# Seven products of a pair collected in one PSUM bank, with ScalarE copies between them

## The chip, the cores and the metric

The kernel runs on one core of a Trainium2 chip. The metric is the device time of one execution in microseconds (us). TensorE (PE) multiplies, VectorE (DVE) adds and subtracts, ScalarE (ACT) casts, copies and evaluates functions, GpSimd (POOL) and SyncE (SP) here mainly issue DMAs. Each engine runs its own list of instructions in order, and lists wait for one another by semaphores.

## The reference

One decoder block over x of 1024 tokens by 1024 channels in float32. What is computed, cut to its core:

```
h = rms_norm(x, norm_g)
proj = h @ w_in          # u, g_rnn, q, k, v, g_attn, m_rnn, m_attn
y_rnn  = rg_lru(conv4(u)) * silu(g_rnn)
y_attn = sliding_window_attention(rope(q), rope(k), v, sinks) * silu(g_attn)
merged = sigmoid(m_rnn) * (y_rnn @ w_rnn_out) + sigmoid(m_attn) * (y_attn @ w_attn_out)
out = rms_norm(x + merged @ w_o, final_norm_g)
```

## The kernel before

**Products.** A float32 product is made of three float32r matmuls: each operand is split into a high part (an ACT cast, L427) and a low part (a DVE subtraction, L428), and high by high, high by low, low by high are summed in PSUM (L508 to L510). Each matmul is 128 rows by 512 columns. The weights come in pairs of 128-column units. A `Pair` is a product of a 256 by 1024 by a 1024 by 1024 matrix in 2 by 2 blocks, done by Strassen's scheme in Winograd's form: seven block products instead of eight, each of 4 x 3 matmuls (`product`), so 84 matmuls a pair. Left factors are A11, A12, A22, S1, S2, S3, S4 (S1 to S4 are sums of blocks, by DVE), right factors B11, B21, T2, T3, T1, T4, B22 (T1 to T4 are sums of the right matrix's blocks, also made and split on DVE and ACT, once for all pairs of that right matrix).

**One pair.** `Pair.run` uses five PSUM banks a to e. Product 0 (A11 B11) goes to a, and ACT copies it to SBUF (`p1`, L517). Product 1 (S2 T2) goes to b, and DVE adds the copy: u2 = b + c1. Product 2 (A12 B21) goes onto a, which then is the first result block. Product 3 (S3 T3) goes to c: u3 = c + u2. Product 4 (S1 T1) goes to d: c22 = d + u3. Product 5 (A22 T4) goes to e: c21 = e + u3. Product 6 (S4 B22) goes onto d, after c22 has read it: c12 = d + u2. All the additions are DVE's (L435).

**Stages.** After the norm and the transposes of x (right matrix h), two pairs of the merge gate are done in the plain form (`fd`). Then 24 pairs run over h: `ug` (u and g_rnn together, followed by the recurrence `lru`), `mr`, `ma`, `ga` (gates), `k`, `v`, `q`. Between them stand the 32 attention units `a00` to `a37` (scores, softmax on ACT and DVE, values). Then come four pairs `zr` with y_rnn as the right matrix and four pairs `za` with y_attn as the right matrix (`z_seven`, `comb_from`: y is loaded back from DRAM, for `za` also multiplied by the gate sg, `YB`; then T1 to T4 are made and 28 buffers are split). `z_tail` multiplies each result by its gate (`tz`) and adds both branches. Last is the product with w_o (`o`), the residual, the norm and the store.

**What sets the order.** `Plan` records every operation with what it reads and writes, and places them one after another on the engines by estimated times, priorities (`prio` with offsets such as `lru`, `ztl`, `comb`) and counts of buffers allowed per class (`raw`, `wc`, `B`, `Y`, `ld`). `TUNE['orders']` gives the sequence of pairs and attention units. The instructions of each engine then stand in exactly that order. `ahead` ties the loading of y to a product that stands so many products before `zr0` or `za0` (`gzr`, `gza`). The functions of ACT belong to table sets, and the planner's order decides how often a table is loaded. PSUM has eight banks.

Of the kernel before, what the change touches and what calls it, by code (L numbers as in the profile page):

```python
# [12 lines left out]
AF = mybir.ActivationFunctionType  # L13
# [23 lines left out]
    'zy': 7,  # L37
    'zg': 3,
    'raw': 4,
    'raws': 9,  # L40
    'S': 4,
    'wc': 10,
    'B': 12,
    'psw': 67,
    'psk': 0,
    'Y': 8,
    'ld': 9,
    'lds': 21,
    'kv': 8,
    'kvs': 4,  # L50
    'qt': 4,
    'qts': 1,
    'P': 17,
    'AO': 22,
    'AOs': 12,
    'xo': 24,
    'lru0': 136,
    'xos': 11,
    'prep': 256,
    'att': 73,  # L60
    'val': 13,
    'gate': 1500,
    'lru': -1570,
    'qk': -147,
    'comb': 346,
    'ztl': -331,
    'xof': 47,
    'gzr': 21,
    'gza': 21,
    'gwo': 11,  # L70
    'gxo': 3,
    'gt': -6,
    'seven': 'ra',
    'mgd': 0,
# [268 lines left out]
def hybrid_block_kernel(ctx: ExitStack, tc: tile.TileContext, x, wall, wo, bd, vec, gfin,  # L343
# [20 lines left out]
    def buf(cls, shape=None, dt=F32, name=None):  # L364
        return Buf(sp, "s2", cls, shape or [P, HF], dt, name or cls)
# [95 lines left out]
    class Pair:  # L461
# [3 lines left out]
        def __init__(self, i, comb, prio=None, cls="raw", by="POOL"):  # L465
            self.i, self.comb, self.prio, self.cls, self.A = i, comb, TUNE["prep"] if prio is None else prio, cls, {}
            self.W = {}
            self.by = by

        def raw(self, name):  # L470
            if name not in self.A:
                t = self.A[name] = buf(self.cls, name=name)
                b = ("A11", "A21", "A22", "A12").index(name)
# [3 lines left out]
        def left(self, name):  # L477
            raw, prio, A = self.raw, self.prio, self.A
            if name[0] != "S":
                return raw(name)  # L480
            if name == "S1":
                return A["S1"]
            src = A[name] = buf("S", name=name)
            if name == "S2":
                s1 = A["S1"] = buf("S", name="S1")
                tt(s1, raw("A21"), raw("A22"), ADD, prio)
                tt(src, s1, raw("A11"), SUB, prio)
# [26 lines left out]
        def p1(self):  # L514
            self.a, self.c1 = bank("pair"), slot("p1")
            self.product(0, self.a, "A11", "B11", True)
            ACT(lambda q: q.copy(self.c1.t, self.a.t), HF, [self.a], [self.c1])  # L517

        def p2(self):
            self.product(2, self.a, "A12", "B21", False)  # L520
# [716 lines left out]
```

## Time and profile before

| | us |
|---|---|
| median of 3 runs | 901.39 (901.3 to 901.75) |
| profiled execution, its own time | 901.53 |
| span of the profile | 899.8 |
| PE busy | 874.7 (97%) |
| DVE busy | 774.4 (86%) |
| ACT busy | 599.9 (67%) |
| POOL busy | 72.9 (8%) |

The span runs from the first to the last instruction, the device time is a little more. Busy times count an instruction from its start to its end. Matmuls overlap their followers, so a matmul of 0.39 us is followed by the next after about 0.23 us; elementwise instructions of DVE and ACT overlap by about 0.09 us as well.

### The profile page before, as it was taken

The numbers are of one execution on the slowest core, as the hardware profiler recorded it, in microseconds if no ns is written. First come the engines' busy times: TensorE is split into PE (matmuls) and PEld (weight loads), VectorE is DVE, ScalarE is ACT, GpSimd is POOL, SyncE is SP. The second block draws the span as 40 slices with busy tenths as digits, with TensorE's granted clock in tenths as the row PEclk, the third lists the DMA queues.
The fourth block names the chain that finished last, engine by engine and source line by source line (L and its number), as shares of the span: only waits on it lengthen the run. The fifth ranks groups of instructions, "written<-read, shape, count | busy, mean of one in ns | idle before, by whom it ended". The sixth has DMA issues, their size and how long they took to land.

```text
span 899.8 us, 13035 instructions
## 1 busy us (share of the span) xinstructions
PE 874.7 (97%) x4088; PEld 721.8 (80%) x4088; DVE 774.4 (86%) x1579; ACT 599.9 (67%) x1232; POOL 72.9 (8%) x131
## 2 busy tenths in 40 slices
PE   4999999999999999999999999999999989999996
PEld 3778888878887888888888888888888868888885
DVE  6996999999996998888888888789999999897643
ACT  7655996996847777896498999999751444334000
POOL 2101010101000010011000000001100200000000
PEclk9999999999999999999999999999999979999999
DMA  9202146345641665256666445553857621682311
GB/s 327 104 34 83 58 119 173 111 140 145 164 129 48 194 193 139 72 138 213 171 173 188 132 130 176 146 158 89 268 184 244 207 74 50 208 297 78 117 47 47
DMA packets 86884, 129.75 MB, mean 144 GB/s; under 512 B 10656, under 2 KB 40224, under 8 KB 86816
## 3 DMA queue, kind: packets, MB, share of 16 engines
q1 hardware_dynamic: 77216, 97.47, 35.0%
q0 software_dynamic: 9600, 31.46, 12.1%
q8 instruction: 32, 0.52, 0.2%
q14 instruction: 36, 0.29, 0.1%
HBM read 87.21 MB, written 41.68 MB: 143 GB/s over the span
## 4 chain that ended last, share of the span: by engine, by line
PE 63%; DVE 3%; ACT 3%; issue 1%; DVEq 0%
PE pair L508 15%; PE pair L509 15%; PE pair L510 15%; PE o L569 3%; PE o L570 3%; PE o L568 3%; PE ps_s L899 3%; PE ptp L933 3%; PE po L947 1%; PE po L946 1%; ACT sm L914 1%; ACT sm L922 1%; DVE wl L428 1%; DVE cu L728 0%; ACT ph L427 0%
## 5 line engine op out<-in xcount | busy, mean ns | idle before, releaser
L418 POOL DMA_DIRECT2D A<-in_wall_dram x120 | 64.5, 538 | 676.6 <-PE pair L510 169.4
L427 ACT CAST wh<-S 128x512 fp32r<-128x512 f32 x128 | 78.3, 616 | 41.2 <-DVE S L435 27.6
L428 DVE TENSOR_TENSOR wl<-S,wh 128x512 fp32r<-128x512 f32 x128 | 87.6, 686 | 7.9 <-ACT wh L427 6.7
L435 DVE TENSOR_TENSOR c<-pair,u 128x512 f32<-128x512 f32 x96 | 65.6, 686 | 7.0 <-PE pair L510 6.4
L428 DVE TENSOR_TENSOR wl<-A,wh 128x512 fp32r<-128x512 f32 x96 | 65.9, 687 | 1.7 <-ACT wh L427 1.1
L427 ACT CAST wh<-A 128x512 fp32r<-128x512 f32 x96 | 59.3, 617 | 12.1 <-PE pair L510 6.3
L914 ACT ACTIVATE sm<-sm,nm 128x256 f32<-128x256 f32 (+1 forms) x128 | 61.9, 487 | 1.8 <-DVE nm L907 1.6
L922 ACT ACTIVATE sm<-sm,dn 128x256 f32<-128x256 f32 (+1 forms) x128 | 53.9, 489 | 1.8 <-DVE dn L919 0.9
L907 DVE CUSTOM_DVE_ANT_0 sm<-ps_s,mask_t,sink_t 128x256 f32<-128x256 f32 (+1 forms) x128 | 53.8, 459 | 1.0 <-PE ps_s L899 1.0
L509 PE MATMUL pair<-B21l,wh 128*128 128x512 f32 x128 | 51.2, 400 | 1.1 <-DVE B21l L428 1.1
L508 PE MATMUL pair<-B11h,wh 128*128 128x512 f32 x128 | 51.7, 404 | 0.5 <-DVE B12l L424 0.5
L508 PE MATMUL pair<-B21h,wh 128*128 128x512 f32 x128 | 51.9, 406 | 0.3 <-ACT B21h L427 0.3
L509 PE MATMUL pair<-T2l,wh 128*128 128x512 f32 x128 | 50.0, 391 | 1.9 <-DVE T2l L428 1.9
L563 ACT ACTIVATE sd<-ss,eps_t 128x1 f32<-128x1 f32 x16 | 4.3, 289 | 71.1 <-DVE ss L561 71.1
L508 PE MATMUL pair<-B22h,wh 128*128 128x512 f32 x128 | 51.0, 398 | 0.8 <-DVE c L435 0.8
L510 PE MATMUL pair<-B21h,wl 128*128 128x512 f32 x128 | 50.9, 398 | 0.0
L508 PE MATMUL pair<-T3h,wh 128*128 128x512 f32 x128 | 50.7, 396 | 0.0
L508 PE MATMUL pair<-T4h,wh 128*128 128x512 f32 x128 | 50.7, 396 | 0.0
L508 PE MATMUL pair<-T1h,wh 128*128 128x512 f32 x128 | 50.6, 396 | 0.0
L509 PE MATMUL pair<-B11l,wh 128*128 128x512 f32 x128 | 50.5, 394 | 0.0
L510 PE MATMUL pair<-B11h,wl 128*128 128x512 f32 x128 | 50.3, 393 | 0.0
L508 PE MATMUL pair<-T2h,wh 128*128 128x512 f32 x128 | 50.1, 392 | 0.0
(222 smaller groups left out, 2606.2 us busy)
## 6 DMA issues: line engine op xcount, KB each, us to landing
A<-in_wall_dram POOLq DMA_DIRECT2D x120, 256.0 KB, 3.2
qt<-st_q SPq DMA_DIRECT2D x32, 256.0 KB, 3.5
xt<-in_x_dram SPq DMA_DIRECT2D x16, 256.0 KB, 5.4
A<-in_wall_dram SPq DMA_DIRECT2D x16, 256.0 KB, 5.4
tm_r<-tm SPq DMA_DIRECT2D x16, 256.0 KB, 2.2
yr_dr<-tg SPq DMA_DIRECT2D x16, 256.0 KB, 2.2
K<-st_k SPq DMA_DIRECT2D x32, 128.0 KB, 3.6
st_q<-qh SPq DMA_DIRECT2D x32, 128.0 KB, 2.9
```

The costliest lines, as they stand in the source:

```text
L418: pl.op([("POOL", 1000.0)], reads, writes, lambda e: nc.gpsimd.dma_start(dst(), src()), prio, move=move)
L427: ACT(lambda e: e.copy(h(), src()), cols, reads, wh, prio)
L428: (DVE if psum else EW)(lambda e: e.tensor_tensor(l(), src(), h().bitcast(F32), op=ALU.subtract), cols, list(reads) + list(wh), wl, prio)
L435: (eng or EW)(lambda e: e.tensor_tensor(dst.t, a.t, b.t, op=op), HF, [a, b], [dst], prio)
L508: nc.tensor.matmul(ps.t, h.t[:, w], bh.t, start=start and k == 0, stop=False, **kw)
L509: nc.tensor.matmul(ps.t, h.t[:, w], bl.t, start=False, stop=False, **kw)
L510: nc.tensor.matmul(ps.t, l.t[:, w], bh.t, start=False, stop=k == 3, **kw)
L568: nc.tensor.matmul(ps.t, h.t[:, w], bh.t, start=start, stop=False)
L569: nc.tensor.matmul(ps.t, h.t[:, w], bl.t, start=False, stop=False)
L907: DVE(lambda v, ps=ps, j=j, h=h, s=s: v.tensor_tensor_reduce(s.t[:, j, :], ps.t[:, j, :], att["mask"].t[:, 256 - w : 256], scale=-0.125, s ...
L914: ACT(lambda e, h=h, s=s, j=j: e.activation(s.t[:, j, :], s.t[:, j, :], AF.Exp, scale=-1.0, bias=nm.t[:, h : h + 1], accum_out=dn.t[:, h : ...
L922: ACT(lambda e, h=h, s=s, j=j: e.activation(s.t[:, j, :], s.t[:, j, :], AF.Identity, scale=dn.t[:, h : h + 1]), w, [(s, j), dn], [(s, j)], ...
```

## The change

`Pair.run` now uses three banks a, b and d and another order of products. Products 0 (A11 B11), 1 (S2 T2), 3 (S3 T3) and 5 (A22 T4) are all accumulated in bank a, one after another; after each of the first three ACT copies the bank to SBUF (c1, u2, u3). Product 4 (S1 T1) stands second, in d. Product 2 (A12 B21) goes to b and DVE adds c1 (c11). c22 = d + u3 and c12 = d + u2 remain. After product 5, bank a holds the other result block itself. So DVE has three sums a pair where it had five, and ACT three copies where it had one. `S1` is made as a left factor of its own. For the `ug` pairs the two unit rows are exchanged (`turned`: the block list is permuted and `lru` unpacks `g, (u0, u1)`), and in `lru` the two SiLU activations of g stand ahead of the recurrence (`sil`) instead of at its end. The table `TUNE` has other counts and offsets throughout and another sequence of pairs and attention units. `pre` is 0, so the branch `first` isn't taken.

```diff
-    'B': 12,      'wc': 10,     'raw': 4,   'lru': -1570,  'ztl': -331,  'gzr': 21,  'gza': 21,
+    'B': 11,      'wc': 11,     'raw': 5,   'lru': -1261,  'ztl': -483,  'gzr': 28,  'gza': 49,
...
-    'orders': 'ug3 ug4 k0 ug5 ug7 q1 ug6 q0 ug0 ug1 v0 a00 ...
+    'orders': 'k0 ug3 ug0 v0 q1 ug5 ug2 ug4 ug7 ug6 q0 a00 ...
...
+            self.turned = i < U_MR
...
-                b = ("A11", "A21", "A22", "A12").index(name)
+                b = (("A21", "A11", "A12", "A22") if self.turned else ("A11", "A21", "A22", "A12")).index(name)
...
-            self.p1()
-            a, c1 = self.a, self.c1
-            b, c, d, e = (bank("pair") for _ in range(4))
+            a, b, d = (bank("pair") for _ in range(3))
             u2, u3 = slot("u2"), slot("u3")
-            c12, c21, c22 = slot("c12"), slot("c21"), slot("c22")
-            self.product(1, b, "S2", "T2", True)
-            tt(u2, b, c1, ADD, 0, DVE)
-            self.p2()
-            self.product(3, c, "S3", "T3", True)
-            tt(u3, c, u2, ADD, 0, DVE)
+            c12, c22 = slot("c12"), slot("c22")
+            first = TUNE["pre"]
+            self.product(0, a, "A11", "B11", True)
+            c1 = b if first else slot("c1")
+            ACT(lambda q: q.copy(c1.t, a.t), HF, [a], [c1])
             self.product(4, d, "S1", "T1", True)
+            self.product(1, a, "S2", "T2", False)
+            ACT(lambda q: q.copy(u2.t, a.t), HF, [a], [u2])
+            self.product(2, b, "A12", "B21", not first)
+            c11 = b
+            if not first:
+                c11 = slot("c11")
+                tt(c11, b, c1, ADD, 0, DVE)
+            self.product(3, a, "S3", "T3", False)
+            ACT(lambda q: q.copy(u3.t, a.t), HF, [a], [u3])
             tt(c22, d, u3, ADD, 0, DVE)
-            self.product(5, e, "A22", "T4", True)
-            tt(c21, e, u3, ADD, 0, DVE)
+            self.product(5, a, "A22", "T4", False)
             self.product(6, d, "S4", "B22", False)
             tt(c12, d, u2, ADD, 0, DVE)
-            return [[a, c12], [c21, c22]]
+            return [[c11, c12], [a, c22]]
...
-        (u0, u1), g = C
+        g, (u0, u1) = C
...
+        tgs = []
+        for gg in g:
+            tgs.append(slot("tg"))
+            ACT(lambda e, tg=tgs[-1], gg=gg: e.activation(tg.t, gg.t, AF.Silu), HF, [gg], [tgs[-1]], TUNE["sil"], tset=SILU)
...
-            gg = g[h]
-            ACT(lambda e, tg=tg, gg=gg: e.activation(tg.t, gg.t, AF.Silu), HF, [gg], [tg], tset=SILU)
```

In both built programs PE has 4088 matmuls and the first 268 of them stand alike. The table loads of ACT are 64 in the program before and 43 in the changed one; copies at the end of products are 32 and 96; the DVE instructions of L435 (L437 in the changed one) are 424 and 360.

ACT at the first pair, before (`p1` is the copy of bank a, `wh` and `uh` casts, `cu` and `edge` parts of the recurrence):

```order
L517 COPY p1_883<-pair_634 128x512
L427 CAST wh_894<-S4_520 128x512
L427 CAST wh_914<-A11_509 128x512
L716 COPY edge_924<-pair_634 128x3
L724 ACTIVATE cu_926<-pair_634,vec_t_99 128x512
L427 CAST wh_939<-S2_555 128x512
```

The same place in the changed program (`c1`, `u2`, `u3` are the copies of the one bank; the pair is `k0` here, and `qh` its cast):

```order
L522 COPY c1_883<-pair_634 128x512
L429 CAST wh_898<-A11_267 128x512
L429 CAST wh_916<-S1_554 128x512
L525 COPY u2_922<-pair_634 128x512
L429 CAST wh_937<-S2_559 128x512
L429 CAST qh_948<-c11_942 128x512
L429 CAST wh_962<-A12_528 128x512
L532 COPY u3_971<-pair_634 128x512
```

One copy has become three, with two or three casts between them.

DVE around the end of `zr3`, before (`c12` is the last sum of that pair; `T2l` are the low parts of the right factor that `za0` uses second; `wl`, `S4`, `tz` belong to pairs and tails):

```order
L435 TENSOR_TENSOR c12_8364<-pair_8271,u2_8226 128x512
L428 TENSOR_TENSOR T2l_8371<-T2_8313,T2h_8322 128x512
L428 TENSOR_TENSOR T2l_8380<-T2_8327,T2h_8373 128x512
L428 TENSOR_TENSOR wl_8389<-A22_8188,wh_8387 128x512
L1032 SCALAR_TENSOR_TENSOR tz_8334<-tz_8334,pair_8143 128x512
L1032 SCALAR_TENSOR_TENSOR tz_8338<-tz_8338,c12_8364 128x512
L1032 SCALAR_TENSOR_TENSOR tz_8343<-tz_8343,c21_8332 128x512
L435 TENSOR_TENSOR S4_8405<-A12_8200,S2_8263 128x512
L1032 SCALAR_TENSOR_TENSOR tz_8352<-tz_8352,c22_8303 128x512
L428 TENSOR_TENSOR T2l_8410<-T2_8336,T2h_8382 128x512
L428 TENSOR_TENSOR T2l_8414<-T2_8345,T2h_8412 128x512
```

The same place in the changed program, where `za0` uses T1 second and T2 third:

```order
L437 TENSOR_TENSOR c12_8331<-pair_8132,u2_8192 128x512
L1033 SCALAR_TENSOR_TENSOR tz_8252<-tz_8252,c12_8331 128x512
L430 TENSOR_TENSOR wl_8341<-A22_8155,wh_8326 128x512
L430 TENSOR_TENSOR T1l_8347<-T1_8051,T1h_8319 128x512
L430 TENSOR_TENSOR T1l_8351<-T1_8058,T1h_8349 128x512
L430 TENSOR_TENSOR T1l_8355<-T1_8067,T1h_8353 128x512
L437 TENSOR_TENSOR S4_8362<-A12_8164,S2_8219 128x512
L430 TENSOR_TENSOR T2l_8366<-T2_8141,T2h_8357 128x512
L430 TENSOR_TENSOR T2l_8375<-T2_8148,T2h_8368 128x512
L430 TENSOR_TENSOR wl_8382<-S4_8362,wh_8373 128x512
L430 TENSOR_TENSOR T2l_8389<-T2_8174,T2h_8377 128x512
L430 TENSOR_TENSOR T2l_8393<-T2_8201,T2h_8391 128x512
```

Behind `c12` stood four tails and two of the four T2 parts; now one tail stands there, and three of the four T1 parts and all four of T2 follow.

PE from the last matmul of `zr3` to `za0`, before (8358 and 8393 are banks of `za0`, 8478 the next pair's):

```order
L510 MATMUL pair_8271<-B22h_7865,wl_8214 128x512
L508 MATMUL pair_8358<-B11h_8212,wh_8246 128x512
...
L508 MATMUL pair_8393<-T2h_8322,wh_8269 128x512
...
L509 MATMUL pair_8393<-T2l_8410,wh_8269 128x512
...
L508 MATMUL pair_8358<-B21h_8423,wh_8295 128x512
...
L508 MATMUL pair_8478<-B11h_8212,wh_8468 128x512
```

And in the changed program (8262, 8337 and 8442 are banks a, d and b of `za0`, 8418 is bank a of `za1`):

```order
L511 MATMUL pair_8132<-B22h_7873,wl_8157 128x512
L509 MATMUL pair_8262<-B11h_8228,wh_8159 128x512
...
L509 MATMUL pair_8262<-B11h_8270,wh_8159 128x512
...
L509 MATMUL pair_8337<-T1h_8279,wh_8221 128x512
...
L510 MATMUL pair_8337<-T1l_8347,wh_8221 128x512
...
L509 MATMUL pair_8262<-T2h_8357,wh_8237 128x512
...
L510 MATMUL pair_8262<-T2l_8389,wh_8237 128x512
...
L509 MATMUL pair_8418<-B11h_8153,wh_8384 128x512
...
L509 MATMUL pair_8442<-B21h_8403,wh_8260 128x512
L510 MATMUL pair_8442<-B21l_8422,wh_8260 128x512
...
L509 MATMUL pair_8418<-B11h_8270,wh_8384 128x512
...
L509 MATMUL pair_8442<-B21h_8424,wh_8260 128x512
```

Half of A11 B11 of `za0` now stands ahead of the end of `zr3`, and A11 B11 of `za1` stands between the T2 and the B21 product of `za0`.

## Rows read from the trace of the kernel before

**Rows 1.** The page's parts 1 and 2: busy shares, slices.
```profile
span 899.8 us, 13035 instructions
...
PE 874.7 (97%) x4088; PEld 721.8 (80%) x4088; DVE 774.4 (86%) x1579; ACT 599.9 (67%) x1232; POOL 72.9 (8%) x131
...
PE   4999999999999999999999999999999989999996
...
PEclk9999999999999999999999999999999979999999
```

**Rows 2.** Timeline of PE at za0: start us, us, engine, line, op.
```profile
723.83 0.39 PE L508 MATMUL pair<-T2h,wh 128*128 128x512 f32 x1
...
725.19 0.39 PE L508 MATMUL pair<-T2h,wh 128*128 128x512 f32 x1
727.47 0.50 PE L509 MATMUL pair<-T2l,wh 128*128 128x512 f32 x1 [1.89 <-DVE T2l L428]
```

**Rows 3.** Waits of PE: waiter, releaser, total us, times, longest.
```profile
PE pt L636 <- DVE xt L629: 8.8, 2, 8.5
PE fd L568 <- DVE B11l L424: 2.6, 1, 2.6
PE pair L509 <- DVE T2l L428: 1.9, 1, 1.9
PE fd L569 <- DVE B21l L424: 1.2, 1, 1.2
PE pair L509 <- DVE B21l L428: 1.1, 2, 0.8
PE pair L508 <- DVE c L435: 0.8, 2, 0.5
```

**Rows 4.** Windows: length, engines' busy us (instructions), PEclk, DMA share, GB/s.
```profile
650.00:700.00 50.00, 50.00 (x221) 40.99 (x220) 49.20 (x82) 18.34 (x33) 3.21 (x6) 1.00 0.67 211
...
725.00:728.00 3.00, 1.11 (x5) 0.64 (x4) 3.00 (x7) 0.14 (x1) 0.00 (x0) 1.00 0.00 0
728.00:739.00 11.00, 9.58 (x23) 6.32 (x22) 11.00 (x20) 5.83 (x11) 1.08 (x2) 0.53 0.15 48
```

**Rows 5.** Timeline of DVE at za0, same columns as PE's.
```profile
721.31 0.69 DVE L435 TENSOR_TENSOR c<-pair,u 128x512 f32<-128x512 f32 x1
...
726.73 1.29 DVE L428 TENSOR_TENSOR T2l<-T,T2h 128x512 fp32r<-128x512 f32 x2
...
732.14 1.90 DVE L428 TENSOR_TENSOR B21l<-YB,B21h 128x512 fp32r<-128x512 f32 x3
733.94 0.69 DVE L435 TENSOR_TENSOR S<-A,A 128x512 f32<-128x512 f32 x1
```

**Rows 6.** Groups by form: line, op, names, shapes, count, busy us, mean ns, idle.
```profile
L435 DVE TENSOR_TENSOR c<-pair,u 128x512 f32<-128x512 f32 x96 | 65.6, 686 | 7.0 <-PE pair L510 6.4
...
L517 ACT COPY p<-pair 128x512 f32<-128x512 f32 x32 | 18.6, 582 | 15.9 <-PE pair L510 15.8
L748 ACT ACT_TABLE_LOAD x14 | 18.0, 1283 | 0.3
```

**Rows 7.** Timeline of ACT: a table load.
```profile
12.64 1.28 ACT L696 ACT_TABLE_LOAD   x1
13.93 0.21 ACT L696 ACTIVATE ee<-ab 128x8 f32<-128x8 f32 x1
```

**Rows 8.** Window over the attention stretch, columns as in the windows above.
```profile
420.00:640.00 220.00, 219.89 (x1163) 185.20 (x1162) 187.77 (x493) 195.36 (x501) 17.83 (x34) 1.00 0.56 162
```

**Rows 9.** Groups of ACT in that stretch: the copies.
```profile
L517 ACT COPY p<-pair 128x512 f32<-128x512 f32 x8 | 4.7, 583 | 0.1
```

**Rows 10.** Timelines of PE and of ACT in that stretch.
```profile
508.69 0.40 PE L510 MATMUL pair<-B11h,wl 128*128 128x512 f32 x1
...
518.00 0.57 ACT L517 COPY p<-pair 128x512 f32<-128x512 f32 x1
```

More of the change, by code (lines that the diff above doesn't have):

```diff
@@ L36 @@
     'pen': 99999,
-    'zy': 7,
-    'zg': 3,
-    'raw': 4,
+    'zy': 6,
+    'zg': 5,
+    'raw': 5,
     'raws': 9,
     'S': 4,
-    'wc': 10,
-    'B': 12,
-    'psw': 67,
+    'wc': 11,
+    'B': 11,
+    'psw': 65,
     'psk': 0,
     'Y': 8,
-    'ld': 9,
-    'lds': 21,
+    'ld': 11,
+    'lds': 25,
     'kv': 8,
-    'kvs': 4,
+    'kvs': 5,
     'qt': 4,
-    'qts': 1,
-    'P': 17,
+    'qts': 0,
+    'P': 19,
     'AO': 22,
-    'AOs': 12,
+    'AOs': 14,
     'xo': 24,
-    'lru0': 136,
-    'xos': 11,
-    'prep': 256,
+    'lru0': -216,
+    'xos': 10,
+    'prep': 250,
     'att': 73,
-    'val': 13,
+    'val': 95,
     'gate': 1500,
[L63 to L72, printed above, removed]
+    'lru': -1261,
+    'qk': -197,
+    'comb': 345,
+    'ztl': -483,
+    'xof': 71,
+    'gzr': 28,
+    'gza': 49,
+    'gwo': 10,
+    'gxo': 2,
+    'gt': -1,
     'seven': 'ra',
+    'pre': 0,
+    'sil': 100,
     'mgd': 0,
[3 rows of a table removed]
[3 rows of a table added]
 }
@@ L480, in left @@
                 return raw(name)
+            src = A[name] = buf("S", name=name)
             if name == "S1":
[L482 to L487, printed above, removed]
+                tt(src, raw("A21"), raw("A22"), ADD, prio)
+            elif name == "S2":
+                tt(src, A["S1"], raw("A11"), SUB, prio)
             elif name == "S3":
@@ L512, in product @@
                 PE(go, 3, [h, l, bh, bl], [ps] + [mark(self.i, n)] * (k == 0))
[L514 to L520, printed above, removed]
         def run(self):
-            self.p1()
-            a, c1 = self.a, self.c1
-            b, c, d, e = (bank("pair") for _ in range(4))
+            a, b, d = (bank("pair") for _ in range(3))
             u2, u3 = slot("u2"), slot("u3")
-            c12, c21, c22 = slot("c12"), slot("c21"), slot("c22")
-            self.product(1, b, "S2", "T2", True)
-            tt(u2, b, c1, ADD, 0, DVE)
-            self.p2()
-            self.product(3, c, "S3", "T3", True)
-            tt(u3, c, u2, ADD, 0, DVE)
-            self.product(4, d, "S1", "T1", True)
+            c12, c22 = slot("c12"), slot("c22")
[3 more added lines that the diff above has]
+            ACT(lambda q: q.copy(c1.t, a.t), HF, [a], [c1])
+            self.product(4, d, "S1", "T1", True)
+            self.product(1, a, "S2", "T2", False)
[7 more added lines that the diff above has]
+            ACT(lambda q: q.copy(u3.t, a.t), HF, [a], [u3])
             tt(c22, d, u3, ADD, 0, DVE)
-            self.product(5, e, "A22", "T4", True)
-            tt(c21, e, u3, ADD, 0, DVE)
+            self.product(5, a, "A22", "T4", False)
             self.product(6, d, "S4", "B22", False)
             tt(c12, d, u2, ADD, 0, DVE)
-            return [[a, c12], [c21, c22]]
+            return [[c11, c12], [a, c22]]
     CN = ("B11", "B21", "T2", "T3", "T1", "T4", "B22")
@@ L746, in lru @@
                 pm.append(ps)
-            r, i, t, tg = (slot(n) for n in ("r", "i", "t", "tg"))
+            r, i, t = (slot(n) for n in ("r", "i", "t"))
+            tg = tgs[h]
             ACT(lambda e, r=r, ps=pm[0]: e.activation(r.t, ps.t, AF.Sigmoid, bias=col(V_BA + c)), HF, [pm[0], vec_t], [r],
```

6 rows, old and new, of the table TUNE are left out of this document.

## The prediction

> **What bounds the kernel now.** I read the busy shares first. PE is busy for 874.7 of the 899.8 us of the span, DVE 774.4, ACT 599.9, and PE's row of slices is 9 nearly everywhere [rows 1]. In full stretches the matmuls stand at a fixed distance: six in 1.36 us, so 0.227 us each [rows 2]. So only PE's holes can be won. The list of PE's waits says where they are [rows 3]: 8.8 us for the first normalised x, 2.6 and 1.2 us for the first right factors (`fd`), all at the start; then 1.9 and 1.1 us for the low parts T2l and B21l, and 0.8 us in two waits for a sum `c`. The granted clock is 9 in every slice but the one near 730 us, a 7 [rows 1].
>
> The hole near 730 us is the start of `za0`, the first pair on y_attn. From 725 to 739 us PE ran 5 and 23 matmuls, and in the later part at a granted clock of 0.53, between its two levels of 1.2 and 2.4 GHz [rows 4]. At 0.227 us, 14 us hold 61.7; 33.7 are missing, and that is **7.6 us lost**, more than the idle time alone. DVE was busy through all of it and for 49.2 of 50 us in the window from 650 us on [rows 4], so its queue is what PE waited for. The order of before lists the queue: after the last sum of `zr3`, which starts at 721.31, two T2l, a split, four tails and a sum, and then the last two T2l, at 726.73 [rows 5]. One starts each 0.60 us (three from 732.14 to 733.94). PE came to T2 at 723.83, was through its first two parts at 725.19 and could use the third at 727.47, 0.05 us after that part's end [rows 2].
>
> **Part 1: DVE loses two sums in each pair.** There are 32 pairs [rows 6], by the copies `p`; 64 sums go. At a distance of 0.60 us that is 38 us of DVE's time (44 us by the 686 ns of one [rows 6], but neighbours overlap). On the path this counts only where DVE is waited for, so I walk `za0` again with the changed order.
>
> Time 0 is the end of `zr3`'s last matmul on PE. For the walk I count matmuls from there at 0.227 us, and DVE's instructions at 0.60 us each, plus 0.1 us until the last has landed. First the walk is tried on the order of before: DVE starts `c12` at 0; the third T2l is its tenth instruction, ready at 6.1 us; PE would use it as the 19th matmul, at 4.3 us; 1.8 us late (the trace: 1.9 [rows 3]). The last B21l is the 21st, at 12.7 us, against the 34th matmul, 7.7 us: 5.0 late. The worst is the last T1l, the 40th, 24.1 us against 17.9 us (79th matmul): **6.2 us late**, of the 7.6 us that the windows give; the rest I put down to the lower clock.
>
> Now the changed order. DVE comes to `c12` a little late: the sum c22 of `zr3` needs the copy u3, which follows T3's end (30 matmuls, 6.8 us before time 0) by 0.6 us, and c12 stands 11 instructions behind c22: -6.1 + 6.6 = 0.5 us. From there:
> - second T1l: fourth instruction, 3.0 us, against the 10th matmul (2.3 us): 0.7 late;
> - third T2l: 11th, 7.2 us, against the 25th (5.7 us): 1.5 late;
> - first B21l: 19th, 12.0 us, against the 40th (9.1 us): **2.9 late**;
> - T3l, T4l, B22l (33rd, 46th, 55th): 20.4, 28.2, 33.6 us against the 79th, 112th, 136th matmul (17.9, 25.4, 30.9 us): 2.5, 2.8, 2.7.
>
> So DVE catches up no further, and falls back no further, and PE loses 2.9 us instead of 7.6. The gain is **4.7 us**. Its ends: nothing lost (7.6 us) if DVE is less full there than one instruction each 0.60 us; and no gain at all if the clock falls again as it did in [rows 4].
>
> **Part 2: product 6 waits less.** The two waits for `c` (0.8 us in all [rows 3]) are those of S4 B22 on bank d until c22 has read it. Before, one product (12 matmuls, 2.7 us) lay between; now the copy u3 and c22 have T4 and usually 9 matmuls of the next pair (4.8 us). I take **0.8 us** off; the other end is 0.
>
> **Part 3: one bank, three copies.** Each copy now stands between two products of bank a: PE may write only when ACT has read. Between them PE has 12 matmuls of another bank (2.72 us) after c1 and u2 and mostly 9 (2.04 us) after u3. A copy takes 0.58 us [rows 6]; behind one cast or another elementwise instruction of about 0.6 us it ends 1.3 us after the product. That fits under 2.04 us. I take **0** for the 96 copies. The lower end is 0 too, since the copy c1 held nothing up before. The upper end is the rival below. ACT gets 64 x 0.58 = 37 us and loses 21 table loads (64 to 43) of 1.283 us [rows 6], 27 us: 10 us more on an engine that works 600 of 900. First what the row shows: the load at 12.64 is followed by its activation at 13.93, 1.29 us later [rows 7]. The Trainium skill's page "ScalarE: Activation LUTs", section "What ACT_TABLE_LOAD costs", gives some 2.66 us for each switch, a drain of 1.38 us included; this trace shows no such drain, but by the page the estimate for ACT would be 56 us off and 37 on, so less queue before the copies, and I would put the slow rival below at 0.12.
>
> **Part 4: the rest.** The matmuls are the same 4088. The start up to the 268th is the same, so the 8.8, 2.6 and 1.2 us of [rows 3] stay. The end (product with w_o, last norm) has the same instructions. The `turned` rows and the moved SiLU lie on ACT and DVE behind running products, whose cover is PE's unbroken work in [rows 4, 8]; without that cover a SiLU would cost what a copy does, about 0.6 us a time. The other sequence of pairs and loads moves DMAs on SP and POOL; DMA share is 0.67 at most in the windows shown [rows 4, 8], and I cost it at 0.
>
> **Sum.** 901.5 (the profiled execution's own time, 0.1 us above the median of 901.39) - 4.7 - 0.8 = **896.0 us**.
>
> **The rivals.**
>
> *The hole closes (B).* If DVE arrives at `zr3`'s end with no queue, all 7.6 us and the 0.8 us go: 901.5 - 8.4 = 893.1 us, and with some of the small gaps that PE has around waits in the middle, 890. For it: 38 us less work for DVE before and in the last stages, and y_attn is fetched earlier (`gza` 49 products ahead instead of 21). Against it: it is still one long row of DVE work, and the planner now has y_attn multiplied while `zr` runs.
>
> *The hole stays (C).* If the waits of part 1, though shorter, let the granted clock drop again, PE runs for 11 us at 0.53, as in [rows 4], where 23 matmuls took the time of 48. Then 4.7 us of gain are eaten: 901.5 - 0.8 = 900.7 us. For it: it happened in this place. Against it: the two waits for `c` left the clock at 9 in [rows 1], and 2.9 us are spread over three gaps.
>
> *ACT comes late (D), slower than before.* In the attention stretch from 420 to 640 us ACT is busy for 195.4 of 220 us [rows 8], with the softmax in front of the copies. One is in [rows 10]: A11 B11 ends at 508.9 us, its copy starts at 518.0, 9.1 us later. Before, that cost nothing, for PE wrote elsewhere; now PE would stand after 2.72 us. Eight of the copies lie in this stretch [rows 9]. If one copy of each came half as late as that one, 4.5 us, PE would lose 8 x 1.8 = 14 us: 910 us; at the full lag 8 x 6.4 = 51 us. It decides from a lag of 3.4 us on: 0.7 us x 8 take back the 5.5 us gained. For it: ACT's load there, and three copies in place of one. Against it: the attention matmuls stand between the products too and lengthen the cover, and the first pair's order has only casts between the copies. The Trainium skill's page "PSUM — Partial Sum Buffer", section "PSUM bank collisions raise a hardware error", says that two engines must never be in one bank and the same partitions at once, so that every access has to be fenced by semaphores. By that rule no copy can run beside the next product of bank a, which is this rival's ground; no row shows a collision.
>
> That the change doesn't do what it says can be left aside: the order shows three copies and three sums.
>
> **How the numbers follow.** Forecast (A, 893 to 899.5) 0.50, B 0.22, C 0.13, D 0.15. A measurement of this kernel can tell 0.2% (1.8 us) from no change, so faster means under 899.6. Faster: 0.49 of A and B's 0.22, 0.71. Same: C and the edge of A, 0.13. Slower: D and a little of C, 0.16. The range goes from 890 to 903.5: it takes in A, C and nearly all of B, and leaves out D.
>
> **What would show it.** In the profile after: PE's waits for T1l, T2l and B21l near 730 us at some 3 us in all and PEclk at 9 there (A); no such waits (B); a slice of PEclk at 7 or so (C); PE's waits on the copies `c`, `u` of bank a in the attention stretch (D). DVE's busy time should fall by 38 to 44 us, ACT's rise by about 10. I am wrong if PE's idle time shows up anywhere else, above all before `zr0`, where DVE makes the right factors while attention ends.

## The result, and the profile after

The changed kernel takes **907.74 us** (median of 6 runs, 904.88 to 909.61) against 901.43 us for the kernel before in the same session (6 runs, 900.63 to 902.34). The ratio is 1.0067, with a 95% interval of 1.005 to 1.0084: slower by 6.3 us, where 896.0 us had been forecast, with 903.5 as the upper end. The profiled execution took 907.43 us, the one of before 901.5.

The page after, parts 1 and 2: span, busy us, and the rows of PE, of the granted clock and of the DMA share in 40 slices.

```profile
span 905.7 us, 13028 instructions
...
PE 873.6 (96%) x4088; PEld 720.3 (80%) x4088; DVE 737.8 (81%) x1515; ACT 604.9 (67%) x1275; POOL 73.0 (8%) x131
...
PE   4999999999999999999999998999999989999996
...
PEclk9999999999999999999999999999999999999999
DMA  9314621752222773776424546545655631682211
```

Against [rows 1]: PE has the same work. DVE is down by 36.6 us (38 forecast), ACT up by 5.0 (10 forecast). The 7 in the clock's row near 730 us is gone. New is the 8 in PE's row at slice 25, around 555 us. So the change did what it says to the engines, and the time still went up. (One bank collects four of the seven products, 0, 1, 3 and 5; the title says all seven.)

PE's waits after (waiter, releaser, total us, times, longest), those that answer to [rows 3] or are new:

```profile
PE ptp L934 <- ACT sm L923: 2.9, 1, 2.9
PE pair L510 <- DVE T1l L430: 2.7, 2, 2.2
...
PE pair L511 <- DVE wl L430: 1.1, 1, 1.1
...
PE pair L509 <- ACT u L532: 0.8, 2, 0.5
PE po L948 <- DVE pw L430: 0.8, 1, 0.8
```

The waits at the start stand nearly as before (`xt` 9.5 us for 8.8). T2l, B21l and `c` of [rows 3] are gone; T1l and `wl` stand in their place at za0. The 2.9 us of `ptp` lie in the attention stretch, where the kernel before had no such row.

Three windows: za0 in the kernel before, za0 after, and the attention stretch after, which answers to [rows 8].

```profile
720.00:760.00 40.00, 36.69 (x141) 28.51 (x140) 39.97 (x68) 19.87 (x36) 2.15 (x4) 0.87 0.16 53
```
```profile
720.00:760.00 40.00, 36.02 (x153) 28.11 (x153) 38.47 (x64) 21.74 (x41) 4.30 (x8) 1.00 0.38 129
...
420.00:640.00 220.00, 215.11 (x1107) 179.51 (x1107) 170.37 (x442) 193.91 (x488) 16.64 (x31) 0.99 0.49 142
```

In both kernels only products of pairs run from 720 to 760 us, 0.227 us apart [rows 2], so their count is the progress made: 153 for 141. za0 gained 12 x 0.227 = 2.7 us. In 420 to 640 us PE stands idle for 4.9 us; before it was 0.1 [rows 8]. Add 3.4 us at half the clock there (below), which cost 1.7 us. **The loss is in the attention stretch, 6.5 us of it against 2.7 gained at za0**; between 50 and 420 us PE idles 2.0 us against 0.9 before. That makes about 4.9 of the 5.9 us between the two profiled executions. Of the rest, 0.6 us lies at the start, where the two programs are still alike: PE's 268th matmul begins at 72.72 us, before at 72.09.

The largest hole is one piece. ACT's timeline after (start us, us, engine, line, op, names, idle time before and its releaser), then the chain that ended last, then the stores' way from issue to landing, and the window over it:

```profile
544.77 0.19 ACT L918 ACTIVATE es<-es 128x4 f32<-128x4 f32 x1
548.00 0.58 ACT L952 COPY pvt<-po 64x512 f32<-64x512 f32 x1 [3.04 <-DMA sg_dr<-tga]
```
```profile
540.85 7.05 DMA sg_dr<-tga
...
550.20 0.44 PE ptp L934 x2
```
```profile
DMA to landing us min/median/max: 2.0/4.1/7.3
```
```profile
540.00:555.00 15.00, 12.13 (x54) 9.86 (x53) 9.06 (x32) 11.88 (x37) 0.00 (x0) 0.89 1.01 312
```

ACT wants to copy `po` into a tile `pvt` at 544.96 us and stands until 548.00: the SBUF buffer that `pvt` was given still holds a SiLU output `tga`, whose store, issued at 540.85, takes 7.05 us to land. The new sequence computes the eight `tga` of the pairs ga3 and ga1 behind one table load and stores them in one burst, while K, Q and V are fetched; the DMA share is 1.01 there. Behind ACT wait the softmax and, from 547 to 550 us, PE. This was theory 1: **the burst of stores**. Theory 2 was rival D of the prediction in a wider form: **the new form of the pairs** itself, its copies on ACT above all, is what the attention stretch can't carry.

### The profile page after: what moved, and what is told of

The parts are those of the page before. It is cut to its first block, busy times and chain, and to the rows that moved or that the text cites. A ratio compares the mean times of both kernels' runs of the same rounds, so it can differ in the third digit from the quotient of the medians.

```text
span 905.7 us, 13028 instructions
## 1 busy us (share of the span) xinstructions
PE 873.6 (96%) x4088; PEld 720.3 (80%) x4088; DVE 737.8 (81%) x1515; ACT 604.9 (67%) x1275; POOL 73.0 (8%) x131
## 4 chain that ended last, share of the span: by engine, by line
PE 61%; DVE 15%; ACT 13%; DMA 5%; issue 4%; SPq 1%; DVEq 0%; ACTq 0%
PE pair L509 14%; PE pair L511 14%; PE pair L510 14%; PE o L567 3%; PE o L566 3%; PE o L568 3%; ACT sm L915 2%; DVE wl L430 2%; DVE cu L730 2%; PE ps_s L900 2%; ACT sm L923 2%; ACT wh L429 2%; PE ptp L934 2%; DVE hs L763 1%; PE fd L567 1%
## 5 line engine op out<-in xcount | busy, mean ns | idle before, releaser
L510 PE MATMUL pair<-T1l,wh 128*128 128x512 f32 x128 | 50.1, 392 | 2.7 <-DVE T1l L430 2.7
L437 DVE TENSOR_TENSOR c<-pair,u 128x512 f32<-128x512 f32 x64 | 43.7, 682 | 10.0 <-PE pair L511 5.8
L430 DVE TENSOR_TENSOR pw<-ptp,ph 128x512 fp32r<-128x512 f32 x60 | 40.4, 682 | 12.9 <-ACT ph L429 12.5
```

The source lines that it names most:

```text
L430: (DVE if psum else EW)(lambda e: e.tensor_tensor(l(), src(), h().bitcast(F32), op=ALU.subtract), cols, list(reads) + list(wh), wl, prio)
L437: (eng or EW)(lambda e: e.tensor_tensor(dst.t, a.t, b.t, op=op), HF, [a, b], [dst], prio)
L510: nc.tensor.matmul(ps.t, h.t[:, w], bl.t, start=False, stop=False, **kw)
```

## The experiments

Every kernel ran beside the kernel before (900.5 to 901.2 us there). "Sequence held" means that each engine's instructions keep their order.

| run | what differs | us | ratio, 95% interval |
|---|---|---|---|
| e1_struct | new form, table of before | 928.06 | 1.0268 to 1.0311 |
| e2_table | old form, table of after | 917.92 | 1.0162 to 1.0203 |
| e3_ownbuf | after, `pvt` in buffers of its own | 906.12 | 1.0032 to 1.0068 |
| e4_dvecopy | after, u2 and u3 copied by DVE, planned anew | 939.39 | 1.0408 to 1.0439 |
| e5_parted | after, the burst parted | 906.85 | 1.0049 to 1.0078 |
| e6_tail | before, new form in za0 to za3 | 902.58 | 1.0008 to 1.0026 |
| e7_one_number | before, one number of the table | 902.56 | 1.0009 to 1.0028 |
| e8_z_pairs | before, new form in zr0 to za3 | 900.64 | 0.9985 to 1.0002 |
| e9_vcopy | after, u2 and u3 copied by DVE, sequence held | 923.54 | 1.0232 to 1.0262 |
| e10_dose | before, 64 copies more on ACT, sequence held | 938.95 | 1.0406 to 1.0434 |
| e11_tail_table | e8 with nine numbers of the new table | 906.77 | 1.0048 to 1.0076 |
| e12_slots | after, other buffers, sequence held | 908.37 | 1.0067 to 1.0094 |
| e13_before_slots | before, other buffers, sequence held | 900.91 | 0.9989 to 1.0008 |
| e14_slots30 | e12 with 30 us for 8 | 938.05 | 1.0391 to 1.0429 |
| e15_land3 | after, planned with stores 3 us longer | 912.59 | 1.0117 to 1.015 |
| e16_land1 | after, planned with stores 1.5 us longer | 906.22 | 1.0046 to 1.0088 |
| e17_ga_pairs | before, new form in ga0 to ga3 | 916.36 | 1.0152 to 1.0208 |
| e18_ug_pairs | before, new form in ug0 to ug7 | 913.32 | 1.012 to 1.0155 |

### The two halves of the change

e1 is the changed kernel with the numbers and the order of pairs of the kernel before; e2 is the kernel before with those of the changed one, and with its old SiLU, loads and pairs.

```diff
-    'wc': 11, 'raw': 5, 'zg': 5, 'val': 95, ... 'orders': 'k0 ug3 ug0 ...'
+    'wc': 10, 'raw': 4, 'zg': 3, 'val': 13, ... 'orders': 'ug3 ug4 k0 ...'
```

> The edit alone: pairs run with three sums and three copies on one bank, while the table of numbers, and with it the sequence of the work, is that of the kernel before (64 additions less on VectorE, 64 copies more on ScalarE). Theory 1, the loss comes from the new sequence (eight SiLU outputs stored in one burst, and a PSUM copy at 545 us that waits for a buffer still being stored): without that sequence 896 to 900 us, no wait of ScalarE on a store of tga above 1 us, 500 to 600 us without the 8 us of TensorE lost there. Theory 2, the copies on bank a make ScalarE come late in the attention stretch: 905 us or more, with TensorE waits behind ScalarE's copies u summing to 4 us or more.

> The other half: pairs run as before (five sums, one copy), but with the table of numbers and the sequence of pairs and loads of the changed kernel. Theory 1 (the sequence): 904 to 910 us, with TensorE waiting 2 us or more in one piece in the attention stretch for ScalarE or a transfer. Theory 2 (the copies): 900 to 903 us, as the kernel before.

Measured: 928.06 and 917.92 us, both far above the whole change. Each theory missed one half: theory 1 said that the form alone is cheap, theory 2 that the table alone is. So the table is no passenger of the change. With the new form it takes 20 us off, with the old one it adds 17: it goes with the form. e1's waits for the copies `u` sum to 2.2 us, where theory 2 had asked for 4 or more. Where the halves lose is told apart by one window, 500 to 620 us, in which pairs run among the attention units. In turn: the kernel before, e2, e1, and the changed kernel.

```profile
500.00:620.00 120.00, 119.89 (x660) 101.08 (x659) 100.13 (x293) 116.84 (x315) 6.98 (x13) 1.00 0.48 138
```
```profile
500.00:620.00 120.00, 119.99 (x636) 100.09 (x635) 101.02 (x266) 114.18 (x296) 9.11 (x17) 1.00 0.53 160
```
```profile
500.00:620.00 120.00, 109.97 (x578) 91.42 (x577) 85.73 (x265) 107.05 (x297) 5.90 (x11) 0.96 0.44 126
```
```profile
500.00:620.00 120.00, 115.57 (x604) 96.71 (x602) 94.36 (x254) 104.56 (x279) 7.51 (x14) 0.99 0.51 151
```

With the old form PE is full under either table (119.89 and 119.99 of 120); with the new form it is not under either (109.97 and 115.57). In this window the new table halves the loss of the new form; it does not cause it. Nor does e1 need a burst of stores for its loss: neither ACT nor DVE waits for a store there for 0.3 us or more. e2 loses its 17 us in other places, between 200 and 500 us (10.2 us of PE's idle time) and at za0. The kernels are at different points of their work in one window, so the rows tell how full PE was, not how far it came.

### The hole at 547 us

e3 leaves each instruction in its place and gives `pvt` a pool of two buffers. e5 puts the four SiLU of ga3, and their stores, some 20 us earlier, where their inputs are ready.

```diff
+    own = ctx.enter_context(tc.tile_pool(name="own", bufs=2))
...
+        tmp.pool, tmp.own = own, "pvt"
```
```diff
-        for _, i, e in self.run():
+        at = max(k for k, x in enumerate(seq) if x[1] in need) + EARLY
+        seq[at:at] = moved
+        for _, i, e in seq:
```

> The changed kernel with every instruction in its place; only the PSUM copy pvt of the attention has two buffers of its own, so that it no longer takes the buffer of a tile that is on its way to DRAM. Theory 1: the 3.0 us hole of TensorE at 547 us goes, and with it part of the half clock behind it (551 to 554 us): 902 to 905 us. Theory 2 (copies on bank a): within 1 us of the changed kernel, 907 to 908 us. If the transfers of the burst are late for others than pvt too, the hole moves to the next tile that waits for a store and the time stays.

> The changed kernel with its sequence kept, but for the four SiLU outputs of pair ga3 and their four stores: they stand some 20 us earlier, where their inputs are ready, so that the burst of eight stores becomes two of four (two more table loads on ScalarE, 2.6 us). Theory 1 (the burst keeps buffers that the attention needs next): the hole of TensorE at 547 us (3.0 us, with 3.4 us at half clock behind it) falls under 1 us and the time to 902 to 904 us. Theory 2 (ScalarE itself is late, with the copies on bank a): the two table loads make it no better, 907 us or more.

e3: 906.12 us, the interval overlapping that of the changed kernel. The wait passed to the next tile that was given such a buffer, as the last sentence of the expectation has it, and PE still stands for 2.4 us:

```profile
DVE wl L431 <- DMA sg_dr<-tga: 3.6, 1, 3.6
```

e5: 906.85 us. Its windows, over the old hole and over the place where the SiLU went:

```profile
540.00:555.00 15.00, 15.00 (x85) 12.88 (x84) 11.55 (x38) 13.28 (x36) 1.61 (x3) 1.00 0.88 267
515.00:525.00 10.00, 7.33 (x34) 5.64 (x32) 7.16 (x23) 9.70 (x25) 0.54 (x1) 0.83 0.96 285
```

The hole at 547 us is closed (15.00 of 15, clock 1.00), as theory 1 had it. But ACT, busy for 9.70 of the 10 us at the new place with the moved SiLU and the two table loads that the edit adds, holds up PE there for 2.7 us (0 in the changed kernel's trace), and the time stays. The cause of the hole is shown; that it is the cause of the loss is not, and since the edit makes a hole of its own, it isn't excluded either.

### Other buffers, and a planner that knows of the stores

e12 gives each tile a named buffer and reckons one that was stored from as free 8 us later than planned; e14 says 30 us; e13 does e12's to the kernel before. e15 and e16 tell the planner itself that such buffers come free later.

```diff
+                    free.sort()
+                    b.place = free.pop(0)[1]
...
+                    free.append((st + (STORE if o["move"] else 0.0), b.place))
```
```diff
-                b.end = max(fin[i], b.end)
+                b.end = max(fin[i] + (3000.0 if o['move'] else 0.0), b.end)
```

> The changed kernel with all its instructions in the same order on every engine; only the choice among the free SBUF buffers is another: one whose last content was stored to DRAM counts as free 8 us later than planned, so that others are taken first. Theory 1: the waits of ScalarE and VectorE on stores (3.0 us pvt, 1.4 and 1.9 us wl, 0.5 us wh) go, with them TensorE's holes at 547 and 583 us and the half clock behind the first; TensorE's loss in 500 to 600 us falls from 8.3 to about 2 us and the time to 900 to 902.5 us. If buffers are not the cause: 906 us or more.

> Control: the kernel before with the same choice of buffers and its order held. Its trace shows no wait of an engine on a store, so there is nothing to win: 899.5 to 902 us.

> As the run with the other choice of buffers (8 us), but with 30 us: a buffer whose content was stored is taken only when no other is free for that long. Theory 1: no engine waits more than 1 us in one piece for a store, TensorE's loss from 300 to 600 us falls to 5 us or less (11.7 us in the changed kernel, 13.6 us with 8 us) and the time to 900 to 903 us. If waits on stores go and the time stays at 906 us or more, buffers are not what costs; if such waits stay, there are too few free buffers for any choice, and the theory stays open.

> The changed kernel with its table and its operations, planned anew with 3 us more until the buffer of a store counts as free (some 1,100 of 6,400 rows move). Theory 1 (surprise waits on stores): waits of ScalarE and VectorE on stores sum to under 1.5 us, TensorE's loss in 500 to 600 us falls from 8.3 to about 2 us, 899.5 to 903 us. If buffers are not what costs: 906 us or more.

> The same with 1.5 us more, half the dose: by theory 1 between the changed kernel and the run with 3 us, 902 to 906 us; otherwise 906 us or more.

e12's windows: the old hole, and 300 to 420 us; below, its waits on copies of bank a.

```profile
540.00:555.00 15.00, 14.93 (x79) 12.33 (x78) 11.54 (x39) 14.60 (x34) 1.61 (x3) 1.00 0.76 230
300.00:420.00 120.00, 115.69 (x568) 95.80 (x567) 93.03 (x213) 86.34 (x208) 10.19 (x20) 1.00 0.65 181
```
```profile
PE pair L524 <- ACT u L547: 2.5, 3, 1.5
PE pair L524 <- ACT u L540: 2.4, 1, 2.4
```

Again the hole closed and the time stayed, 908.37 us: 4.3 us idle from 300 to 420 us. The longest piece there, 2.4 us up to 317.45 us, is a wait on a store once more: ACT stood until 312.80 us for a buffer whose store to `scr_q` was under way, the copy `u` came late behind it, and PE with it. In all the copies `u` passed 4.9 us on to PE, for 0.8 in the changed kernel. The waits of ACT and DVE on such stores in e12:

```profile
ACT wh L444 <- DMA scr_q<-c: 3.1, 1, 3.1
...
DVE y L969 <- DMA scr_q<-c: 4.3, 2, 3.9
```

e14 is 938.05 us: with 30 us of allowance the buffers that another engine has just read are taken first, and then ACT waits for DVE instead. Its row:

```profile
ACT wh L444 <- DVE wl L445: 32.9, 27, 2.7
```

e13 is unchanged at 900.91, so in the order of the kernel before the same choice costs nothing. e15 and e16 gave 912.59 and 906.22 us. The larger dose was slower, against theory 1's order, and e15 has its hole elsewhere: eight operations of a recurrence on DVE ran ahead of the attention's `y`, and PE stood for 5.5 us.

```profile
500.50 1.11 PE L934 MATMUL ptp<-ident,sm 128*128 128x128 f32 x4 [5.50 <-DVE y L954]
```

Five kernels took the wait on stores away or moved it, and none came out faster than 906 us. That doesn't refute theory 1, since none was free of such waits: the longest of ACT or DVE was 3.6 us in e3, 2.4 in e5, 3.9 in e12, 1.2 in e15 (3.2 us in all, where its expectation had asked for under 1.5) and 1.7 in e16. What speaks against it as the whole loss is e1, and e17 below: PE loses 10 us and more from 500 to 620 us there, and no such wait of 0.3 us or more stands in that window ahead of its holes.

### The form, stage by stage

These put the new form into some pairs of the kernel before, with its table (e11 with nine numbers of the new one). PE's rows are those of before up to the first of these pairs in e17, at 508 us, and in e6 and e8 up to 669 and 605 us, somewhat ahead of the pairs. e7 is the control for moving rows at all.

```diff
         def run(self):
+            if self.i in SOME:
+                return self.run3()
             self.p1()
```
```diff
-    'wc': 10,
+    'wc': 11,
```

> The kernel before, with its table and its sequence up to za0 unchanged row by row; only the four pairs za0 to za3 run with three sums and three copies. Were part 1 of the prediction right about its place, the 7.6 us hole at za0 becomes 2 to 3.5 us as in the changed kernel, the clock does not fall there, and the time is 895 to 898 us. Rival: the new order of products wants T1 so early that TensorE waits as long as before: 900 to 902 us.

> A control: the kernel before, its pairs and operations unchanged; one number of the table is another one, that of the changed kernel (wc, the window for split weights, 11 for 10), which moves some 2,000 of the 6,400 rows of the sequence. Theory 3, that the sequence alone, whatever operations it sorts, is worth more than the whole change: 905 us or more. Otherwise within 2 us of the kernel before.

> As the run on the tail, with the eight pairs zr0 to za3 in the new form and the attention stretch as before. VectorE gets rid of 16 more operations of 0.69 us. If the tail's gain is what part 1 says, 895 to 898 us here too; if zr's pairs lose by the new order (their operands wait for ScalarE), 899 us or more.

> As the run with the eight pairs zr0 to za3 in the new form, and besides with the nine numbers of the changed table that act there (prep, comb, ztl, xof, gzr, gza, gwo, gxo, gt); the rows of the attention stretch stay nearly as before. If the hole at za0 shrank in the changed kernel because of these numbers (its operands loaded and combined earlier) and not because of the three sums, it falls here from 6.7 us to about 5 and the time to 897 to 899.5 us; if not, 900 to 901 us.

> The kernel before with its table; only the four pairs ga0 to ga3, which run among the attention units, in the new form; rows up to the first of them as before. If the new form itself is harmful where ScalarE is 0.97 busy (theory 2): 905 us or more, with TensorE waiting for copies u or for the attention's tiles in 500 to 620 us. If it is harmless and only the sequence of the whole counts: within 2 us of the kernel before, as a single changed number was.

> The same with the eight pairs ug0 to ug7, which feed the recurrence and run from the start of the program on, so that nearly all of the sequence moves. Theory 2: little, up to 903 us, since ScalarE is 0.67 to 0.8 busy there. If moving the sequence is what costs: 905 us or more.

The control: 2,000 rows moved cost 1.8 us, so theory 3 of its expectation, that any other sequence is worth more than the change, does not hold for this move. In the last stages the form costs nothing with eight pairs (e8, 900.64) and 1.8 us with four (e6, 902.58); the 895 to 898 us expected of both did not come. za0 in e6, e8 and e11, then in e13, which has the instructions and the order of the kernel before, and in e3, which has those of the changed one:

```profile
720.00:760.00 40.00, 35.92 (x143) 28.26 (x142) 39.73 (x67) 20.17 (x37) 2.70 (x5) 0.91 0.26 91
```
```profile
720.00:760.00 40.00, 37.00 (x149) 29.25 (x148) 39.68 (x67) 19.77 (x37) 2.69 (x5) 0.91 0.22 77
```
```profile
720.00:760.00 40.00, 36.62 (x153) 27.98 (x152) 39.83 (x67) 21.88 (x41) 4.28 (x8) 1.00 0.37 126
```
```profile
720.00:760.00 40.00, 36.57 (x146) 28.46 (x146) 39.97 (x67) 20.17 (x37) 2.15 (x4) 0.91 0.17 55
```
```profile
720.00:760.00 40.00, 37.54 (x162) 29.69 (x161) 39.97 (x67) 22.53 (x42) 4.30 (x8) 1.00 0.30 105
```

Counted as above, the gain over the kernel before is 0.5 us with four pairs, 1.8 us with eight, and 2.7 us with the nine numbers too. But e13 has 146 matmuls where the kernel before has 141, and e3 162 where the changed kernel has 153, with no instruction moved: 1.1 and 2.0 us between two traces of one order. So the counts don't tell the share of the three sums from that of the numbers. e8 did not end earlier for its gain: from its 3550th to its 3760th matmul PE takes 2.4 us more than in the kernel before, 1.0 of them in a wait for `ml` at the product with w_o, where the kernel before had none. e11 (897 to 899.5 us expected) lost 6 us on the way, mostly between 600 and 700 us.

Among the attention units it is otherwise. Four ga pairs alone cost 15.9 us (e17). Its window of the ga pairs, then 27 us of it; last the same 27 us of the kernel before:

```profile
500.00:620.00 120.00, 109.27 (x580) 89.89 (x579) 88.17 (x264) 106.16 (x287) 6.97 (x13) 0.99 0.46 131
535.00:562.00 27.00, 21.65 (x124) 17.01 (x122) 19.93 (x64) 26.80 (x83) 1.61 (x3) 1.00 0.33 93
```
```profile
535.00:562.00 27.00, 27.00 (x143) 22.52 (x142) 22.66 (x61) 26.07 (x58) 2.15 (x4) 1.00 0.54 171
```

PE's groups in those 27 us (line, op, names, count, busy us, idle), of e17 and of the kernel before, attention only:

```profile
L926 PE MATMUL ps_s<-K,qt 128*128 128x256 f32 (+1 forms) x48 | 7.5, 295 | 3.8 <-DVE y L980 3.0 <-DVE nm L934 0.3 <-DVE pw L431 0.3
L960 PE MATMUL ptp<-ident,sm 128*128 128x128 f32 x34 | 5.1, 275 | 1.4 <-DVE pw L431 1.4
L973 PE MATMUL po<-ph,V 128*128 128x512 f32 x9 | 4.1, 455 | 0.1
```
```profile
L899 PE MATMUL ps_s<-K,qt 128*128 128x256 f32 (+1 forms) x29 | 5.3, 294 | 0.0
L933 PE MATMUL ptp<-ident,sm 128*128 128x128 f32 x20 | 3.6, 272 | 0.0
```

In the kernel before, ACT is busy for 26.07 of 27 us and yet PE never waits: 84 of its 143 matmuls are products of pairs, which fill PE while ACT and DVE work on the softmax. In e17 only 24 of 124 are. The attention units stand close together, ACT is at 26.80, PE waits for the attention's own tiles, and the next pair's products follow only afterwards, from 563 to 576 us, where they wait for ACT as well: for split weights, and for a bank that a SiLU still reads.

```profile
PE pair L512 <- ACT tga L993: 2.8, 1, 2.8
...
PE pair L512 <- ACT wh L430: 2.1, 2, 1.2
```

Where ACT is full, what keeps PE going is **pair products at hand as filler**, and in e17 there are fewer of them: 264 of the 580 matmuls from 500 to 620 us, for 317 of 660 in the kernel before. In e1 it is 270 of 578. The changed kernel has 328 of 604, so there the pair products are not fewer, and this account of e17 is not shown to be that of the changed kernel. Of e17's 15.9 us, 10.7 are PE's idle time in this window; the rest is not placed. PE did not wait for the copies `u` in e17 at all, so of theory 2 the place holds and the waits on copies do not. Whether the load of the eight copies more on a full ACT counts, e17 can't tell.

e18 (ug pairs) is 913.32 us with PE at 119.97 of 120 in 500 to 620 us; it loses elsewhere, 5.8 us of it in one wait for a `wl` from 415 to 421 us. It went against theory 2's 903: the new form costs in 500 to 620 us only where its pairs run there, but a moved sequence costs elsewhere.

### The copies' own price

e4 and e9 move u2 and u3 from ACT to DVE, e4 with a new plan, e9 in place. e10 adds two idle copies to each pair of the kernel before.

```diff
-            ACT(lambda q: q.copy(u2.t, a.t), HF, [a], [u2])
+            ACT(lambda q: nc.vector.tensor_copy(u2.t, a.t), HF, [a], [u2])
```
```diff
-            tt(u2, b, c1, ADD, 0, DVE)
+            DVE(lambda v: (v.tensor_tensor(u2.t, b.t, c1.t, op=ADD), nc.scalar.copy(junk_t, b.t)), HF, [b, c1], [u2])
```

> The changed kernel with the second and third copy of each pair (u2, u3) made by VectorE in place of ScalarE, 64 copies that move off ScalarE; the planner then sets the sequence anew. Theory 2 (ScalarE's copies make it late): 900 to 903 us. Theory 1 (the sequence's burst of stores): 904 us or more if the eight SiLU outputs of the two groups are again stored in one burst, 898 to 902 us if the new sequence parts them.

> The changed kernel with its sequence held row by row; only the engine of the 64 copies u2 and u3 is another: VectorE makes them in the place where ScalarE did (some 37 us off ScalarE, 44 us onto VectorE). Theory 2 (ScalarE has no slack left in the attention stretch, so each wait there reaches TensorE): the smaller holes at 415 to 430, 583 and 595 us go and the time falls to 902 to 904 us. Theory 1 (buffers held by stores): the 3.0 us hole at 547 us stays as it is, 906 to 908 us.

> The kernel before with its sequence held; two copies of a PSUM bank per pair are added on ScalarE (64 in all, 37 us, into a buffer that nobody reads), behind the sums u2 and u3, as many as the change adds. Were the copies' price the cause (theory 2), 904 us or more, the loss in 420 to 640 us, where ScalarE was busy 195 of 220 us. Were they free in that sequence, as part 3 of the prediction put it, 900 to 902 us.

All three were much slower (939.39, 923.54, 938.95 us), so neither theory's numbers hold. In e4 PE stands for 16 us between 250 and 320 us, waiting for operands of the recurrence. e9 shows how tight the copy is: made by DVE in the same place, it keeps PE waiting 11 times. It also takes 8 us of load off ACT from 420 to 640 us (185.75 for 193.91), and yet PE idles there for 5.8 us (4.9 in the changed kernel), 1.8 of them in a wait for such a copy. So the copies' load on ACT is not shown to be what costs.

```profile
PE pair L509 <- DVE u L532: 7.5, 11, 1.8
```
```profile
420.00:640.00 220.00, 214.21 (x1111) 179.77 (x1110) 178.69 (x469) 185.75 (x476) 16.26 (x31) 0.99 0.49 143
```

e10 measured something else than it was meant to. I had put each copy behind DVE's sum, and ACT's queue stood still for that sum:

```profile
ACT junk_t L533 <- DVE u L533: 60.1, 28, 6.1
ACT junk_t L530 <- DVE u L530: 43.7, 26, 3.9
```

So its 38 us hold the price of waiting in order, and it decides nothing about the price of the copies themselves.

## Why the prediction was wrong

- **What bounds.** Right: PE's matmuls are unchanged, and what was lost was lost in its holes and in the half clock behind one of them.
- **Part 1, right in its mechanism, its size not settled.** DVE lost 36.6 us (38 said), the hole shrank, the clock stayed full. In this pair of traces the gain is 2.7 us and not 4.7: 40 us hold 176 matmuls, 23 are missing after the change, so PE still lost 5.2 us where the walk had 2.9. The late tiles were T1l (2.7 us) and `wl` (1.1), not B21l. The walk had `c12` 0.5 us and the second T1l 3.0 us behind the end of `zr3`; they came 2.7 and 5.3 us behind it. For 1.3 us of that, in two pieces, DVE stood for a load of the tails, which the walk left out. The longer piece:

```profile
731.05 0.69 DVE L1033 SCALAR_TENSOR_TENSOR tz<-tz,pair 128x512 f32<-128x512 f32 x1 [0.95 <-DMA tz<-tm_r]
```

In e3, the same order without this wait, za0 gains 4.8 us by the same count. That 4.7 had been forecast is no proof of the walk, as two traces of one order differ by up to 2 us here.
- **Part 2, right.** The waits for `c` on product 6, 0.8 us, are gone from PE's list; between 50 and 420 us other holes took more than that.
- **Part 3, right about PE's wait, wrong in what it concluded.** PE waited 0.8 us for copies of bank a, in two waits; 0 was said. But "0 for the 96 copies" took the copy's cover alone into account and spread ACT's work over 900 us ("600 of 900"). In 500 to 620 us ACT was busy for 0.97 in the kernel before, and e17 shows that four pairs in the new form cost 15.9 us there, without one wait for `u`.
- **Part 4, the step that failed.** "The rest" was put at 0, with "PE's unbroken work in [rows 4, 8]" as the cover and the moved DMAs costed at 0. The change itself broke that cover: in the attention stretch, where PE lives on the pairs between the units, it lost 4.8 us of idle time and 1.7 us of clock. More than half of it, 2.9 us and the 1.7 us behind them, followed a wait of ACT on a store: the DMA share of 0.67 "in the windows shown" was of the kernel before, and the new sequence makes a burst of 1.01 there. That the new form empties PE there without such a wait too is shown by e1 and e17; how it does so in the changed kernel stays open.
- **The rivals.** D named the right place and the right engine; its mechanism, PE standing at bank a, came to 0.8 us instead of 14. That its 910 us lie near the 907.7 measured is luck. B and C did not happen. The sentence "I am wrong if PE's idle time shows up anywhere else" is what came true.
- **The range** ended at 903.5, 4 us short, since D, the only slow case, had been left out of it.

With the measured terms in place of the forecast ones: 901.5 - 2.7 + 4.8 + 1.7 + 1.1 (50 to 420 us, part 2 included) = 906.4 us, against 907.43 for the profiled execution. Of the 1.0 us between them, 0.6 us is the later start; 0.4 us is not placed.

**What stays open.** Why PE runs empty among the attention units with the new form: the form's chain (product, copy, next product on one bank) would do it, and so would the fewer banks, the other order of products and the load of more copies on a full ACT. No run parts these; e9 speaks against the last. Nor is it shown how much of the changed kernel's 6.3 us a sequence without waits on stores would give back, since each attempt closed one hole and met another. No version tried beats the kernel before.

## What to carry to other kernels

Where an engine off the critical path is busy for 0.97 of a stretch and PE is still full, as here, PE lives on filler from another stage, and an edit to the filler is an edit to the stretch. Count the filler's matmuls around the hole: 24 of 124 told e17's story, while the whole window of the changed kernel showed no lack. Load on such an engine has to be read by stage: its mean over the span (0.67 here) says nothing about whether 37 us fit. And where numbers that set a sequence are changed together with the code, run code and numbers crosswise and compare one window by stage: the four cells told the form's loss from the table's, while removing single holes told only that each could be removed. Before a difference of 1 or 2 us in one window is read as an effect, look at a second trace of the same order: 141 and 146, 153 and 162 matmuls here.

## What the runs showed that I had not expected

- The landing of the same 256 KB store (`sg_dr`) took 2.0 to 7.3 us in one kernel, the four of 7 us where the DMA share was 0.98 or more. The kernel's planner reckons with 2.5 us when the queues are idle (0.9 to start, 0.7 for the bytes, 0.9 to land) and counts the buffer as free from then on. The Trainium skill's page "DMA: Bandwidth & Descriptors", section "Latency and other measured facts", has a fixed cost of some 2 us for a DMA, mostly the write's receipt, which grows with the load on HBM. The shortest landing agrees with that (2.0 us, the transfer included); no run here parts the receipt from the queueing in the long ones.
- With every engine's instructions in the same order, the choice of SBUF buffers alone moved the time from 907.7 to 938.1 us (e14).
- The granted clock fell behind one stop of PE and not behind another. After the 2.9 us at 547 it was at 1.2 GHz for 3.4 us; at za0, where waits of 2.17 and 1.1 us stand close together and PE is busy for 7.77 of 11 us, it stayed at 2.4 GHz. In the kernel before it had fallen behind a stop of 1.89 us ([rows 2, 4]).

```profile
551.00:554.40 3.40, 3.40 (x13) 2.82 (x12) 1.73 (x5) 3.38 (x12) 0.00 (x0) 0.50 1.02 343
...
732.00:743.00 11.00, 7.77 (x29) 4.78 (x28) 10.92 (x18) 5.47 (x10) 0.00 (x0) 1.00 0.01 2
```
